# A SwiGLU encoder layer on one core: gate and up as seven block products, gated rows through DRAM, and the way down chunk by chunk

## The chip, the cores and the metric

The kernel runs on one core of a Trainium2 chip. It is one launch that reads its inputs from DRAM and writes eight outputs to DRAM. The metric is the device time of that launch in microseconds. The engines have these names in the profile: PE is TensorE's matmul part and PEld its weight loads, DVE is VectorE, ACT is ScalarE, POOL is GpSimd, and SP is SyncE, which here only issues DMA transfers. Each engine works through its own queue in order; semaphores make one engine wait for another.

## The reference

One layer of an encoder for 1,152 tokens (1,024 of a new stream, 128 of running streams) of width 1,024. Two SwiGLU half steps of hidden width 2,816 stand around a mixer of gated DeltaNet heads and trailing means. Cut to what matters here:

```
def swiglu(x, w_gate, w_up, w_down):
    return (jax.nn.silu(x @ w_gate) * (x @ w_up)) @ w_down

x = x + 0.5 * swiglu(rms_norm(x, norm_ffn1[l]), w_ffn1_gate[l], w_ffn1_up[l], w_ffn1_down[l])
m, s_new, conv_new, pool_new = mixer(rms_norm(x, norm_mix[l]), ...)
x = x + m
x = x + 0.5 * swiglu(rms_norm(x, norm_ffn2[l]), w_ffn2_gate[l], w_ffn2_up[l], w_ffn2_down[l])
...
y_prompt = rms_norm(xp, norm_final)
```

Everything is float32. Both half steps have this same shape, and they take most of the time.

## The kernel before

**Layout.** Channels lie on the 128 partitions and tokens along the free axis. The 1,152 tokens are cut in three chunks: chunk 0 of 512 tokens, chunks 1 and 2 of 320. The residual X of all chunks stays in SBUF in eight blocks of channels (`xk(c, k)`, k from 0 to 7). The hidden width is 22 blocks of 128, numbered f.

**A float32 product from three.** TensorE takes operands of a shorter type here (`fp32r`). Every operand is therefore split exactly into a high and a low part: ACT casts the operand (the high part), and DVE or POOL subtracts the cast from the operand (the low part). `mm3` (L172) then does three matmuls: high by high, high by low, low by high. `load_unit` (L156) does this for weights: it loads a unit of 128 x 1024 values (L160, issued by SP), casts it on ACT (L164), and subtracts on DVE or POOL (L165). The raw units go round a ring of three buffers (`r0` to `r2`), the split ones round four (`s0` to `s3`).

**A SwiGLU half step** is `ffn` (L223). `scale_split` applies the norm's weight to X and splits the result; the factor 1/rms of each token, from `rstd_of` (L178), is applied later. The loop at L294 takes f two at a time. For each f and each chunk, `chunk` (L262) sums 8 k-blocks of three matmuls into one bank of PSUM for gate and as many into another for up, so 48 matmuls of the chunk's width. Then DVE multiplies gate by 1/rms (L275), ACT takes SiLU (L276), DVE multiplies up by 1/rms (L277) and the two together (L278), ACT casts the product (L280) and POOL subtracts (L281). The gated rows of two f stay in SBUF. `down_chunk` (L285) multiplies them by the two units of down weights, for each of the eight output blocks d, and DVE adds half of the sum into X (L292). So X is added to eleven times per chunk and half step, and the down weights are loaded and split once.

**Order.** The program is written in the order in which the engines get their work, and a planner (`Products`, L45) fills the mixer's matmul queue by estimated times. The first half step is called at L337, the mixer follows, and the second half step is called at L1062, with the final norm (`final`, L1051) after each chunk. In the loop the next f's gate and up stand ahead of the previous f's down, so TensorE has work while ACT, DVE and POOL finish a gated row.

Of the kernel before, what the change touches and what calls it, by code (L numbers as in the profile page):

```python
# [28 lines left out]
# columns of the constant matrix  # L29
# [8 lines left out]
def trunk(ctx: ExitStack, tc: tile.TileContext, xin, s0, convst, poolst, cm_in, vec_in, small_in,  # L38
          wg1, wu1, wd1, win, wab_in, wpool_in, wout, wg2, wu2, wd2,
          y_out, pdelta, pconv, ppool, sdelta, sconv, spool, x0_out):  # L40
# [3 lines left out]
    class Products:  # L44
        """the tensor engine, with the time that its queue is filled to"""  # L45
# [32 lines left out]
    X = []  # L78
    for c, (o, n) in enumerate(CHUNKS):
        X.append([xpool.tile([P, KT // 2, n], F32, tag=f"x{c}{i}", name=f"x{c}{i}") for i in range(2)])  # L80

    def x_dma(c, dram, back=False):
        """a chunk of the residual to or from DRAM"""
        n = KT // 2 * CHUNKS[c][1]
        for i in range(2):
            t, d = X[c][i].rearrange("p k n -> p (k n)"), dram[:, i * n:(i + 1) * n]
            SY.dma_start(d if back else t, t if back else d)

    def load_x(c):
        o, n = CHUNKS[c]  # L90
        x_dma(c, xin[:, o * KT:(o + n) * KT])

    def xk(c, k):
        return X[c][k // 4][:, k % 4, :]

    vec = const.tile([P, 32 + 48 + 8 + 1], F32, tag="vec", name="vec")
    SY.dma_start(vec, vec_in)
    cm = const.tile([P, C_END], F32, tag="cm", name="cm")

    def cmat(c):  # L100
        return cm[:, c:c + P]

    ident = cmat(C_ID)
# [8 lines left out]
    main = ctx.enter_context(tc.tile_pool(name="main", bufs=1, side="left"))  # L112
    SIZE = dict(h0h=4096, h0l=4096, h1h=2560, h1l=2560, h2h=2560, h2l=2560, g0=3072, t=2560, rb=1152, g12=3840, spare=1664,
                s0=2048, s1=2048, s2=2048, s3=2048, r0=1024, r1=1024, r2=1024)

    def region(tag, dt=F32):
        """one of the parts in which all phases share what the residual leaves of SBUF"""
        return main.tile([P, SIZE[tag]], dt, tag=tag, name=nm(tag))

    for tag in SIZE:  # L120
        region(tag)

    class Slots:
        """rings of buffers cut from regions"""
# [4 lines left out]
        def place(self, t, *items):  # L129
            o = 0  # L130
            for tag, cols, bufs in items:
                for _ in range(bufs):
                    self.mem.setdefault(tag, []).append(t[:, o:o + cols])
                    o += cols

# [14 lines left out]

    W = {}
# [4 lines left out]
    def load_unit(src, e=None):  # L156
        i = W["i"]
        W["i"] += 1
        raw = region(W["raws"][i % len(W["raws"])])
        SY.dma_start(raw, src)  # L160
        raw = raw.rearrange("p (k c) -> p k c", k=KT)
        w = region(W["splits"][i % len(W["splits"])], F32R).rearrange("p (s k c) -> p s k c", s=2, k=KT)
        hi, lo = w[:, 0], w[:, 1]
        A.copy(hi, raw)  # L164
        (e or V).tensor_sub(lo, raw, hi.bitcast(F32))  # L165
        return hi, lo
# [11 lines left out]
    def rstd_of(c, tmp, r, fast):  # L178
        """1 / rms of each token of a chunk, on all partitions"""
# [9 lines left out]
        if fast:  # L189
            # the tokens on partitions for the root, and back  # L190
# [18 lines left out]
    def scale_split(c, wi, hi, lo):  # L209
        """the norm's weight applied, its 1 / rms left for later"""  # L210
# [5 lines left out]
    def h_rows(t, n, m=KT):  # L216
        return [t[:, k * n:(k + 1) * n] for k in range(m)]

    def h_tiles(c):
        return [h_rows(region(f"h{c}{i}", F32R), CHUNKS[c][1]) for i in "hl"]  # L220

# [1 line left out]
    def ffn(wi, wg, wu, wd, finished):  # L223
        weights(("r1", "r2", "r0"), ("s0", "s1", "s2", "s3"))
        fs = Slots()
        fs.place(region("t"), ("nsq", 512, 3), ("su", 512, 1), ("nacc", 512, 1))
        fs.place(region("rb"), *[(f"rb{c}", CHUNKS[c][1], 1) for c in range(3)])
        for r, cs in (("g0", (0,)), ("g12", (1, 2))):
            fs.place(region(r, F32R), *[(f"{t}{c}", CHUNKS[c][1], 3) for c in cs for t in ("ghi", "glo")])

        def tmp(tag):
            return fs.get(tag, 512)

        first = wi == 0
        order0 = (1, 2, 0) if first else (0, 1, 2)
        H, RB = [None] * 3, [None] * 3
        units0 = None

        for c in order0:
            H[c] = h_tiles(c)  # L240
            RB[c] = fs.get(f"rb{c}", CHUNKS[c][1])
        def norm(c):
            scale_split(c, wi, *H[c])
            rstd_of(c, tmp, RB[c], first)

        if first:
            units0 = [load_unit(wg[0])]
            x_dma(1, xin[:, 512 * KT:832 * KT])
            scale_split(1, wi, *H[1])
            units0.append(load_unit(wu[0]))  # L250
            load_x(2)
            SY.dma_start(cm[:, :P], cm_in[:, :P])
            rstd_of(1, tmp, RB[1], True)
            norm(2)
        else:
            for c in order0:
                scale_split(c, wi, *H[c])
                if units0 is None:
                    units0 = load_unit(wg[0]), load_unit(wu[0])
                rstd_of(c, tmp, RB[c], False)  # L260

        def gate_up(f):  # L262
            g, u = units0 if f == 0 else (load_unit(wg[f]), load_unit(wu[f]))
            out = [None] * 3

            def chunk(c, late=None):
                n = CHUNKS[c][1]
                pg, pu = pt("a")[:, :n], pt("b")[:, :n]
                for ps, (whi, wlo) in ((pg, g), (pu, u)):
                    for k in range(KT):  # L270
                        mm3(ps, whi[:, k, :], wlo[:, k, :], H[c][0][k], H[c][1][k], k == 0, k == KT - 1)
                if late:
                    late()
                sg, su = tmp("nsq")[:, :n], tmp("su")[:, :n]
                V.tensor_mul(sg, pg, RB[c])  # L275
                A.activation(sg, sg, AF.Silu)  # L276
                V.tensor_mul(su, pu, RB[c])  # L277
                V.tensor_mul(sg, sg, su)  # L278
                ghi, glo = fs.get(f"ghi{c}", n), fs.get(f"glo{c}", n)
                A.copy(ghi, sg)  # L280
                G.tensor_sub(glo, sg, ghi.bitcast(F32))  # L281
                out[c] = (ghi, glo)
            return out, chunk

        def down_chunk(c, ws, gs):  # L285
            n = CHUNKS[c][1]
            nf = len(ws)
            for d in range(KT):
                po = pt("cd"[d % 2])[:, :n]
                for i in range(nf):  # L290
                    mm3(po, ws[i][0][:, d, :], ws[i][1][:, d, :], gs[i][c][0], gs[i][c][1], i == 0, i == nf - 1)
                V.scalar_tensor_tensor(xk(c, d), po, 0.5, xk(c, d), ALU.mult, ALU.add)  # L292

        for f in range(0, NF, 2):  # L294
            order = order0 if f == 0 else (0, 1, 2)
            g0, do0 = gate_up(f)
            if f == 0 and not first:
                do0(0)
                g1, do1 = gate_up(f + 1)
                do1(0)  # L300
                for do in (do0, do1):
                    do(1)
                    do(2)
            elif f == 0:
                do0(1)
                do0(2)
                g1, do1 = gate_up(f + 1)
                load_x(0)
                SY.dma_start(cm[:, P:], cm_in[:, P:])
                do1(1)  # L310
                scale_split(0, wi, *H[0])
                do1(2)
                do0(0, lambda: rstd_of(0, tmp, RB[0], True))
                do1(0)
            else:
                for c in order:
                    do0(c)
                g1, do1 = gate_up(f + 1)
            ws = [load_unit(wd[f]), load_unit(wd[f + 1])]
            if f + 2 < NF:  # L320
                if f:
                    for c in order:
                        do1(c)
                for c in order:
                    down_chunk(c, ws, (g0, g1))
            else:
                do1(0)
                down_chunk(0, ws, (g0, g1))
                finished(0, tmp)
                do1(1)  # L330
                do1(2)
                for c in (1, 2):
                    down_chunk(c, ws, (g0, g1))
# [815 lines left out]
```

## Time and profile before

| | |
|---|---|
| Time, median of 3 runs | 2291.96 us (2291.74 to 2292.35) |
| Span of the profiled execution | 2290.1 us |
| Profiled execution's own time | about 1.9 us more than its span, 2292.0 us |
| Instructions | 32,077 |
| DMA | 120.98 MB, mean 53 GB/s |

How to read the rows: a window row gives the stretch in microseconds, then the busy time of each engine with its count of instructions, then the mean granted TensorE clock (1.00 is full speed), the busy share of the DMA engines and the GB/s moved. A timeline row gives start and duration in microseconds, engine, line, operation, output and input by the program's names, the shape, a count, and in brackets the idle time before it with what ended it. A group row gives, behind the shape and the count, total busy time in microseconds with the mean of one in nanoseconds, and then the idle time just ahead with its releasers. Matmuls overlap, so the time that one takes from the engine is the distance between starts.

### The profile page before, as it was taken

Reading aid. Unit: us, or ns where it says so; the run is one execution under the profiler, and the core shown is the slowest. Engines: PE = TensorE matmul, PEld = TensorE weight load, DVE = VectorE, ACT = ScalarE, POOL = GpSimd, SP = SyncE. Lnnn points to the kernel's source line nnn. Section 1 sums busy time; section 2 is a strip of 40 time slices with the busy share of each in tenths; the row PEclk is TensorE's granted clock in tenths of the full one; section 3 lists DMA queues with packets and bytes.
Section 4 is the critical chain, followed back from the end, with each engine's and each line's share of the span. In section 5 each row is a group of like instructions: output and inputs, shape, how many; then the busy total and the mean of one; then the engine's idle time right before and its main releaser. Section 6 shows DMA issues by size and latency. Waiting matters only on the chain. (4 is left out here: it accounts for less than half of the span.)

```text
span 2290.1 us, 32077 instructions
## 1 busy us (share of the span) xinstructions
PE 2233.9 (98%) x13087; PEld 2034.3 (89%) x13087; DVE 1193.8 (52%) x2367; ACT 638.0 (28%) x1246; POOL 346.2 (15%) x384
## 2 busy tenths in 40 slices
PE   8999999999999998999999989999999999999997
PEld 7999999999999987787999978999999999999986
DVE  6443344334443477778687687644433443344345
ACT  6111111111112145544554345411121111111113
POOL 1101000100011002222243332100110011000102
PEclk9999999999999999999999999999999999999998
DMA  4111111111111102111222122111111111111102
GB/s 175 46 44 49 37 45 49 38 37 56 37 37 47 37 30 75 47 57 57 90 71 72 57 82 78 47 56 37 38 48 45 37 37 56 38 37 46 47 10 83
DMA packets 36995, 120.98 MB, mean 53 GB/s; under 512 B 5296, under 2 KB 9264, under 8 KB 36080
## 3 DMA queue, kind: packets, MB, share of 16 engines
q1 hardware_dynamic: 36720, 118.70, 16.1%
q8 instruction: 102, 1.67, 0.3%
q0 software_dynamic: 128, 0.25, 0.1%
q14 instruction: 45, 0.37, 0.1%
HBM read 109.31 MB, written 9.62 MB: 52 GB/s over the span
## 5 line engine op out<-in xcount | busy, mean ns | idle before, releaser
L55 PE MATMUL ps_a<-h0h,s 128*128 128x512 f32 (+1 forms) x1504 | 455.3, 373 | 3.7 <-DVE s L165 2.0
L164 ACT CAST s<-r 128x1024 fp32r<-128x1024 f32 x188 | 195.3, 1050 | 720.7 <-PE ps_d L55 477.8
L281 POOL TENSOR_TENSOR g<-t,g 128x512 fp32r<-128x512 f32 (+1 forms) x132 | 155.8, 1180 | 1460.7 <-ACT g L280 1398.5
L55 PE MATMUL ps_c<-g,s 128*128 128x320 f32 (+1 forms) x1584 | 319.5, 336 | 1.6 <-POOL g L281 1.2
L55 PE MATMUL ps_d<-g,s 128*128 128x320 f32 (+1 forms) x1584 | 318.2, 336 | 0.0
L55 PEld LDWEIGHTS ps_a<-h0h,s 128*128 128x128 f32 x1504 | 276.0, 189 | 43.2 <-issue 2.7
L55 PEld LDWEIGHTS ps_c<-g,s 128*128 128x128 f32 x1584 | 260.9, 188 | 24.4 <-POOL g L281 2.1
L55 PEld LDWEIGHTS ps_d<-g,s 128*128 128x128 f32 x1584 | 261.1, 188 | 20.7
L55 PE MATMUL ps_a<-h0l,s 128*128 128x512 f32 (+1 forms) x752 | 278.5, 370 | 0.0
L277 DVE TENSOR_TENSOR t<-ps_b,rb 128x512 f32<-128x512 f32 (+1 forms) x132 | 73.6, 558 | 363.6 <-PE ps_b L55 363.6
L275 DVE TENSOR_TENSOR t<-ps_a,rb 128x512 f32<-128x512 f32 (+1 forms) x132 | 73.6, 558 | 301.7 <-PE ps_a L55 220.2
L165 DVE TENSOR_TENSOR s<-r,s 128x1024 fp32r<-128x1024 f32 x172 | 209.0, 1225 | 41.4 <-ACT s L164 39.5
L55 PE MATMUL ps_b<-h0h,s 128*128 128x512 f32 x704 | 224.3, 389 | 0.0
L55 PE MATMUL ps_a<-h1h,s 128*128 128x320 f32 x944 | 208.0, 315 | 7.5 <-ACT h1h L213 7.5
L280 ACT CAST g<-t 128x512 fp32r<-128x512 f32 (+1 forms) x132 | 67.8, 513 | 383.9 <-DVE t L278 380.9
L55 PEld LDWEIGHTS ps_a<-h1h,s 128*128 128x128 f32 x944 | 157.9, 191 | 9.6 <-ACT h1h L213 7.5
L55 PE MATMUL ps_b<-h2h,s 128*128 128x320 f32 (+1 forms) x736 | 166.3, 308 | 0.0
L55 PE MATMUL ps_b<-h1h,s 128*128 128x320 f32 x704 | 162.5, 310 | 0.0
L55 PE MATMUL ps_a<-h2h,s 128*128 128x320 f32 x704 | 162.3, 309 | 0.0
L292 DVE SCALAR_TENSOR_TENSOR x<-ps_d,x 128x320 f32<-128x320 f32 (+1 forms) x220 | 116.7, 530 | 85.7 <-PE ps_d L55 85.7
L292 DVE SCALAR_TENSOR_TENSOR x<-ps_c,x 128x320 f32<-128x320 f32 (+1 forms) x220 | 116.7, 531 | 82.6 <-PE ps_c L55 82.6
L55 PEld LDWEIGHTS ps_a<-h0l,s 128*128 128x128 f32 x752 | 142.8, 190 | 18.3 <-issue 0.5
(341 smaller groups left out, 3390.7 us busy)
## 6 DMA issues: line engine op xcount, KB each, us to landing
r<-in_wg SPq DMA_DIRECT2D x44, 512.0 KB, 3.7
r<-in_wu SPq DMA_DIRECT2D x44, 512.0 KB, 3.6
r<-in_wd SPq DMA_DIRECT2D x44, 512.0 KB, 3.6
r<-in_win SPq DMA_DIRECT2D x40, 512.0 KB, 3.6
r<-in_wout SPq DMA_DIRECT2D x16, 512.0 KB, 3.6
x<-in_xin SPq DMA_DIRECT2D x4, 640.0 KB, 7.3
out_y<-x SPq DMA_DIRECT2D x16, 160.0 KB, 1.8
x<-in_xin SPq DMA_DIRECT2D x2, 1024.0 KB, 11.2
```

The lines of the kernel that those rows point to most:

```text
L55: self.put(nc.tensor.matmul(out, lhs, rhs, **k), n / 2400 + .003 if lhs.dtype == F32R else max(n, lhs.shape[-1]) / 600)
L164: A.copy(hi, raw)
L165: (e or V).tensor_sub(lo, raw, hi.bitcast(F32))
L275: V.tensor_mul(sg, pg, RB[c])
L277: V.tensor_mul(su, pu, RB[c])
L280: A.copy(ghi, sg)
L281: G.tensor_sub(glo, sg, ghi.bitcast(F32))
L292: V.scalar_tensor_tensor(xk(c, d), po, 0.5, xk(c, d), ALU.mult, ALU.add)
```

## The change

Gate and up of one f are one product of a 2 x 2 block matrix of weights (rows: gate and up; columns: the two halves of the 1,024 input channels, 4 k-blocks each) and a 2 x 2 block matrix of activations (rows: the halves of the channels; columns: two groups of tokens). Eight block products are replaced by seven products of sums and differences of blocks (Winograd's form). The two groups of tokens are the halves of chunk 0 (pair 0, 256 tokens each) or chunks 1 and 2 (pair 1, 320 each).

- `operands` makes, once per pair and half step, seven activation operands from the normed residual, in place in X, and splits each in high and low part: casts on ACT, subtractions alternately on DVE and POOL. X is overwritten, so it is loaded again later from DRAM.
- `gate_up` runs over f. Per f it loads one gate and one up unit, forms four weight sums of 128 x 512 on POOL, casts and subtracts seven half units (`piece`, ACT and DVE, a ring of seven buffers `O0` to `O6`), and does seven products of 4 x 3 matmuls each, in the order B11, B21, then T4 and B22 of the f before, then T2, T1, T3. ACT copies three sums out of PSUM. The gated rows are cast (ACT), subtracted (POOL) and written to DRAM in both parts (`g_keep`).
- The first f of a half step (3 in the first, 4 in the second, for one pair) still go the old way, `plain`, while operands are made. `beside` makes the operands of the other pair during the first pair's loop.
- `fetch` reads the gated rows of a chunk back into SBUF, and `down` then sums all 22 f of one output block in one bank of PSUM with one add into X. The down weights are loaded and split for each chunk, so three times.
- The constant matrix `cm` is loaded after the first half step, and the four pooling histories are loaded by SP in place of POOL's own queue.

The core of the diff:

```diff
+    def operands(p, wi, RS):
...
+        def split(name, src):
+            t = region(f"{reg}{STEPS.index(name)}", F32R)[:, :8 * n].rearrange("p (s k n) -> p s k n", s=2, k=4)
+            A.copy(t[:, 0], src)
+            turn[0] += 1
+            (V if turn[0] % 2 else G).tensor_sub(t[:, 1], src, t[:, 0].bitcast(F32))
...
+        norm(cs[0])
+        yield op
+        split("B11", l1)
+        split("B21", l2)
+        yield op
+        if p:
+            norm(cs[1])
+            yield op
+        V.tensor_sub(l1, l1, r1)
+        V.tensor_sub(r1, r2, r1)
+        split("B22", r2)
+        yield op
+        V.scalar_tensor_tensor(r2, l1, -1.0, r2, ALU.mult, ALU.subtract)
+        split("T2", r2)
+        split("T1", l1)
+        yield op
+        split("T3", r1)
+        V.scalar_tensor_tensor(l2, r2, -1.0, l2, ALU.mult, ALU.subtract)
+        split("T4", l2)
+        yield op
...
+        def piece(src):
+            t = region(f"O{ring[0] % 7}", F32R)
+            ring[0] += 1
+            hi, lo = t[:, :512], t[:, 512:]
+            A.copy(hi, src)
+            V.tensor_sub(lo, src, hi.bitcast(F32))
...
+        def tail(f, u2, s4, al, be, p1, c2, c3):
+            product(al, piece(u2), "T4", False, True)
+            V.scalar_tensor_tensor(p1, al, -1.0, p1, ALU.mult, ALU.mult)
+            go = gs.get("go", 4, n)
+            A.copy(go[:, 0], p1)
+            G.tensor_sub(go[:, 1], p1, go[:, 0].bitcast(F32))
+            product(be, piece(s4), "B22", False, True)
+            V.tensor_add(c2, c2, be)
+            A.activation(c2, c2, AF.Silu)
+            V.scalar_tensor_tensor(c2, c3, -1.0, c2, ALU.mult, ALU.mult)
+            A.copy(go[:, 2], c2)
+            G.tensor_sub(go[:, 3], c2, go[:, 2].bitcast(F32))
...
+        for i, f in enumerate(fs):
...
+            product(al, piece(g1), "B11", True, True)
+            A.copy(p1, al)
+            product(ga, piece(g2), "B21", True, True)
+            V.tensor_add(p1, p1, ga)
+            A.activation(p1, p1, AF.Silu)
+            G.tensor_add(sA, u1, u2)
+            G.tensor_add(sB, sA, g1)
+            if last:
+                tail(*last)
+            product(al, piece(sB), "T2", False, True)
+            A.copy(c2, al)
+            product(be, piece(sA), "T1", True, True)
+            G.tensor_add(sA, g1, u1)
+            product(al, piece(sA), "T3", False, True)
+            A.copy(c3, al)
+            V.tensor_add(c3, c3, be)
+            G.tensor_add(sB, sB, g2)
+            last = (f, u2, sB, al, be, p1, c2, c3)
+            beside(f)
...
+    def down(c, wd, home):
...
+        for ds in groups:
+            ps = {d: pt("d")[:, :n] for d in ds}
+            for f0, m in cuts:
+                for d in ds:
+                    whi, wlo = load_unit(wd[d][:, f0 * P:(f0 + m) * P])
+                    for i in range(m):
+                        f = f0 + i
+                        mm3(ps[d], whi[:, i, :], wlo[:, i, :], home[f][:, :n], home[f][:, n:], f == 0, f == NF - 1)
+            for d in ds:
+                V.scalar_tensor_tensor(xk(c, d), ps[d], 0.5, xk(c, d), ALU.mult, ALU.add)
...
+    op, homes, fetch = half_step(0, wg1, wu1, wd1, g_keep, 1, 3, None)
+    fetch(1, ["B0", "B1", "B2", "B3", "B4", "B5"])
+    gate_up(0, op, range(NF), wg1, wu1, g_keep)
...
+    x_new(1)
+    x_dma(1, xin)
+    fetch(0, ["B6", "x20", "x21"] + [f"A{i}" for i in range(7)] + ["B0", "B1"])
+    x_new(0)
+    x_dma(0, xin)
+    down(1, wd1, homes[1])
+    fetch(2, ["B2", "B3", "B4", "B5", "B6", "B0"])
+    x_new(2)
+    x_dma(2, xin)
+    down(0, wd1, homes[0])
+    down(2, wd1, homes[2])
...
+    down(0, wd2, homes[0])
+    final(0)
+    fetch(2, ["A2", "A3", "A4", "A5", "A6", "B0", "B1"])
+    down(1, wd2, homes[1])
+    final(1)
...
+    down(2, wd2, homes[2])
+    final(2)
```

In the second half step the pairs go in the order 0, 1.

How the queues stand. ACT before, in the steady loop of the first half step (`s` are split weights, `r` raw ones, `t` the gated product, `g0` and `g12` the gated rows):

```order
L164 CAST s2_145_1544<-r0_144_1542 128x1024
L164 CAST s3_147_1549<-r1_146_1547 128x1024
L276 ACTIVATE t_19_99<-t_19_99 128x512
L280 CAST g0_21_101<-t_19_99 128x512
L276 ACTIVATE t_19_99<-t_19_99 128x320
L280 CAST g12_22_102<-t_19_99 128x320
L164 CAST s0_149_1554<-r2_148_1552 128x1024
L276 ACTIVATE t_19_99<-t_19_99 128x320
L164 CAST s1_151_1559<-r0_150_1557 128x1024
```

ACT now, one f of the half chunks' loop (`O` are half units, `Q` the weight sums, `R` raw weights, `x00` the intermediates and `x01` the gated rows). The line before the copy L345 is the cast of T3's half unit, and the lines after it are those of the next f and of the tail:

```order
L308 CAST O4_462_4501<-Q_344_3238 128x512
L345 COPY x00_342_3236<-ps_a_453_4391 128x256
L308 CAST O5_468_4526<-R0_463_4519 128x512
L308 CAST O6_469_4542<-R0_463_4519 128x512
L348 ACTIVATE x00_342_3236<-x00_342_3236 128x256
L308 CAST O0_470_4561<-R3_452_4388 128x512
L323 CAST x01_343_3237<-x00_342_3236 128x256
L308 CAST O1_471_4579<-Q_344_3238 128x512
L327 ACTIVATE x00_342_3236<-x00_342_3236 128x256
L354 COPY x00_342_3236<-ps_a_453_4391 128x256
L329 CAST x01_343_3237<-x00_342_3236 128x256
```

In place of four casts of whole units there are seven of half units per f, each with the name of a sum or of a raw unit, and they stand among copies and SiLUs that wait for products.

POOL had one line in the loop before, the subtraction L281. Now one f of the same loop has six, the four sums between the subtractions of the gated rows:

```order
L360 TENSOR_TENSOR Q_344_3238<-Q_344_3238,R2_523_5179 128x512
L349 TENSOR_TENSOR Q_344_3238<-R1_536_5312 128x512
L356 TENSOR_TENSOR Q_344_3238<-R2_523_5179,R3_524_5180 128x512
L350 TENSOR_TENSOR Q_344_3238<-Q_344_3238,R0_535_5311 128x512
L324 TENSOR_TENSOR x01_343_3237<-x00_342_3236,x01_343_3237 128x256
L330 TENSOR_TENSOR x01_343_3237<-x00_342_3236,x01_343_3237 128x256
```

So a sum stands behind the gated row's subtraction of an earlier f, and the casts of sums on ACT stand behind POOL's sums.

SP before issued nothing but weights in the loop. Now, where the first half step goes from the half chunks' loop to the way down of chunk 1, it has the last gated rows' stores (L333), the fetches of chunk 0's gated rows (L463, `A3` to `A6`), chunk 0's residual (L109) and the down weights (L154):

```order
L333 DMA g_keep0<-x01_343_3237 256x1x256
L463 DMA A4_618_6154<-g_keep0 128x1024 x2
L463 DMA A5_619_6155<-g_keep0 128x1024 x2
L463 DMA A6_620_6156<-g_keep0 128x1024 x2
L109 DMA x00_623_6181<-in_xin 128x2048
L109 DMA x01_624_6182<-in_xin 128x2048
L154 DMA O6_633_6247<-in_wd1 128x1024
```

The first two units of down weights are issued earlier; the third, `O6_633`, stands behind the fetches and the residual.

More of the change, by code (lines that the diff above doesn't have):

```diff
@@ L214, in scale_split @@
             V.scalar_tensor_tensor(lo[k], xk(c, k), w, hi[k].bitcast(F32), ALU.mult, ALU.subtract)
-    def h_rows(t, n, m=KT):
-        return [t[:, k * n:(k + 1) * n] for k in range(m)]
     def h_tiles(c):
[L220 to L232, printed above, removed]
-        first = wi == 0
[L235 to L241, printed above, removed]
+        n = CHUNKS[c][1]
@@ L262, in gate_up @@
[L262 to L333, printed above, removed]
-                    finished(c, tmp)
@@ L337, in trunk @@
-    ffn(0, wg1, wu1, wd1, lambda c, tmp: None)
-    weights(("r0", "r1"), ("s0", "s1", "s2"))
+            x_new(0)
+            x_dma(0, x_keep)
+            for c in (1, 2):
+                x_dma(c, x_keep, True)
+            scale_split(0, wi, *H[0])
+            units = [load_unit(wg[0]), load_unit(wu[0])]
+            norm(0)
+        for f in range(early):
+            plain(f, units if f == 0 else (load_unit(wg[f]), load_unit(wu[f])), cs, H, RS, fs, gk)
+        op = None
+        for op in operands(lead, wi, RS):
+            pass
@@ new lines, in half_step, with beside, fetch @@
+        nxt = [None, None]
+        def beside(f):
+            if f == early and first:
+                x_new(0)
+                x_dma(0, xin)
+            if f == early + 1:
+                nxt[0] = operands(1 - lead, wi, {})
+            if f > early and nxt[0]:
+                nxt[1] = next(nxt[0], nxt[1])
+        gate_up(lead, op, range(early, NF), wg, wu, gk, beside)
+        for op in nxt[0]:
+            nxt[1] = op
+        homes = {}
+        def fetch(c, where):
+            homes[c] = slots(c, where)
+            for f in range(NF):
+                SY.dma_start(homes[c][f].bitcast(F32), gk[c][f])
@@ L921, in trunk @@
     scale_split(0, 1, *hb[0])
-    rstd_of(0, pair(mt("raw", 512), mt("k", 512, slot=1), mt("q", 512, slot=1)), R[0], False)
-    ahead = region("h1h")
+    rstd_of(0, pair(mt("raw", 512), mt("raw", 512), mt("Xs", 512)), R[0], False)
+    ahead = region("B4")
     z2 = ahead[:, 1536:]
@@ L1043, in trunk @@
                 cur[1:] = e
-    X[0] = [xpool.tile([P, KT // 2, 512], F32, tag=f"x0{i}", name=f"x0{i}r") for i in range(2)]
-    x_dma(0, x0_out)
     SY.dma_start(pconv, cout.rearrange("p t j -> p (t j)"))
```

251 lines of the change are left out of this document (184 added, 67 removed).

## The prediction

> **What bounds the kernel now.** I read the page's totals first, then the stages by windows, then single rows.
>
> ```profile
> span 2290.1 us, 32077 instructions
> PE 2233.9 (98%) x13087; PEld 2034.3 (89%) x13087; DVE 1193.8 (52%) x2367; ACT 638.0 (28%) x1246; POOL 346.2 (15%) x384
> ```
> ```profile
> core 0: us, PE busy (x) PEld busy (x) DVE busy (x) ACT busy (x) POOL busy (x), PEclk, DMA share, GB/s
> 8.00:60.00 52.00, 50.31 (x297) 46.74 (x297) 36.66 (x69) 36.58 (x68) 6.88 (x7) 1.00 0.44 163
> 60.00:830.00 770.00, 769.36 (x4410) 708.64 (x4409) 321.91 (x508) 133.88 (x198) 73.37 (x61) 1.00 0.13 41
> 830.00:1460.00 630.00, 600.54 (x3685) 527.08 (x3684) 480.98 (x1229) 312.27 (x743) 174.18 (x232) 0.99 0.21 67
> 1460.00:2260.00 800.00, 798.52 (x4614) 738.33 (x4613) 334.61 (x528) 140.76 (x211) 78.61 (x67) 1.00 0.13 42
> ```
> The windows 60 to 830 and 1460 to 2260 us are the two SwiGLU half steps, and TensorE never pauses there at a granted clock of 1.00; ACT works 17% and POOL 10% of them. So those stages cost what their matmuls cost, and one spacing row prices everything:
>
> ```profile
> 200.04 0.62 PE L55 MATMUL ps_b<-h0h,s 128*128 128x512 f32 x2
> 200.50 0.39 PE L55 MATMUL ps_b<-h0l,s 128*128 128x512 f32 x1
> 200.72 0.62 PE L55 MATMUL ps_b<-h0h,s 128*128 128x512 f32 x2
> ...
> 203.28 0.46 PE L55 MATMUL ps_a<-h1h,s 128*128 128x320 f32 x2
> 203.57 0.31 PE L55 MATMUL ps_a<-h1l,s 128*128 128x320 f32 x1
> 203.72 0.46 PE L55 MATMUL ps_a<-h1h,s 128*128 128x320 f32 x2
> ```
> Three products of 512 columns start every 0.68 us (0.2267 each), three of 320 every 0.44 (0.1467). The 192 extra columns cost 0.080, so 256 columns come to about 0.120 on the same line (estimate; no row has 256; the upper bound is the 320 row's 0.147, the lower half the 512 row, 0.113).
>
> **The change: what TensorE saves.** Gate and up of one f need 48 products of 512 columns for chunk 0 (10.88 us) and 96 of 320 for the others (14.08). Seven block products are 84: of 256 columns 10.08 us, of 320 columns 12.32. The loops run 40 such f for the pair of half chunks and 41 for chunks 1 and 2, so TensorE's floor falls by 40 x 0.80 + 41 x 1.76 = 104 us. The way down keeps its product count.
>
> **What the loop gives the others.** Each f now brings seven half units to cast and subtract, four weight sums on POOL, two subtractions on POOL, two gated casts, two SiLUs and three PSUM copies. Their prices:
>
> ```profile
> L165 DVE TENSOR_TENSOR s<-r,s 128x1024 fp32r<-128x1024 f32 x172 | 209.0, 1225 | 41.4 <-ACT s L164 39.5
> L280 ACT CAST g<-t 128x320 fp32r<-128x320 f32 x88 | 40.5, 460 | 158.6 <-DVE t L278 155.6
> L280 ACT CAST g<-t 128x512 fp32r<-128x512 f32 x44 | 27.3, 620 | 225.3 <-DVE t L278 225.3
> L278 DVE TENSOR_TENSOR t<-t 128x320 f32<-128x320 f32 x88 | 43.4, 493 | 9.9 <-ACT t L276 1.0 <-DVE t L277 0.5
> L278 DVE TENSOR_TENSOR t<-t 128x512 f32<-128x512 f32 x44 | 30.5, 693 | 5.6 <-ACT t L276 1.2
> ```
> ```profile
> 205.46 1.30 POOL L281 TENSOR_TENSOR g<-t,g 128x512 fp32r<-128x512 f32 x1 [10.09 <-ACT g L280]
> 211.94 0.88 POOL L281 TENSOR_TENSOR g<-t,g 128x320 fp32r<-128x320 f32 x1 [5.18 <-ACT g L280]
> 218.98 1.37 POOL L281 TENSOR_TENSOR g<-t,g 128x320 fp32r<-128x320 f32 x1 [6.16 <-ACT g L280]
> ```
> ACT pays 0.62 for 512 columns, 0.46 for 320 and so 0.41 for 256; DVE 0.69, 0.49, 0.42; POOL 1.30, 0.88, 0.74. Per f of chunks 1 and 2 ACT has 7 x 0.62 + 7 x 0.46 = 7.6 us, POOL 4 x 1.30 + 2 x 0.88 = 7.0, DVE about 7.3: each alone fits in 12.32. Before, POOL only answered ACT and nobody waited. Now the queues make a **ring** (the rows of order above show both queues): the sums (POOL) go to the cast of T3's half unit (ACT), which stands ahead of the copy L345; behind this come, in ACT's own order, the casts of B11 and B21, the SiLU, T4's cast, the first gated cast, B22's cast and the second SiLU; then DVE multiplies (L328), ACT casts (L329), POOL subtracts (L330), and behind that stand the next sums. For chunks 1 and 2, with all four sums ahead: 4 x 1.30 + 0.62 + (4 x 0.62 + 5 x 0.46 + 0.49) + 0.88 = 11.97 us. For the half chunks three sums stand ahead: 3.90 + 0.62 + (2.48 + 2.05 + 0.42) + 0.74 = 10.21. Four hand-offs from engine to engine, 0.08 each, follow from the next rows: ACT ends at 218.90 and POOL begins at 218.98. The rings are then 12.3 and 10.5 us, TensorE's floors 12.3 and 10.1: no slack at all.
>
> ```profile
> 217.86 0.49 DVE L278 TENSOR_TENSOR t<-t 128x320 f32<-128x320 f32 x1
> 218.39 1.22 DVE L165 TENSOR_TENSOR s<-r,s 128x1024 fp32r<-128x1024 f32 x1
> ...
> 218.44 0.46 ACT L280 CAST g<-t 128x320 fp32r<-128x320 f32 x1
> ```
> ```profile
> L640 DVE TENSOR_TENSOR h2h<-rb,cm 128x128 f32<-128x128 f32 x16 | 10.4, 708 | 0.1
> L640 DVE TENSOR_TENSOR t<-rb,cm 128x128 f32<-128x128 f32 x16 | 3.6, 285 | 0.1
> ```
> And the ring stretches. POOL's 320 columns took 1.37 us instead of 0.88 while DVE ran L165 (218.39 to 219.61): 0.49 of it is waiting. The other way round too: L640, the same operation, means 708 ns in one buffer and 285 in another, in the mixer, where POOL is busy. [...]
>
> Seven subtractions of 0.69 us run per f; how many fall into POOL's part of the ring no row shows. The bounds are none and four (those of the sums and B22, which follow POOL's work directly); I take two, 1.4 us: **11.9 us per f for the half chunks, 13.7 for chunks 1 and 2**. Against before: 40 x (11.9 - 10.88) = +41, 41 x (13.7 - 14.08) = -16, together **+25 us**. The saving of 104 is gone in the ring.
>
> **Operands beside the loops.** While one pair runs, the other pair's operands are made:
>
> ```profile
> L165 POOL TENSOR_TENSOR s<-r,s 128x1024 fp32r<-128x1024 f32 x16 | 38.8, 2427 | 39.9 <-ACT s L164 39.2 <-ACT r L454 0.3
> L164 ACT CAST s<-r 128x1024 fp32r<-128x1024 f32 x188 | 195.3, 1050 | 720.7 <-PE ps_d L55 477.8 <-PE ps_a L55 133.8 <-issue 82.8
> L184 ACT ACTIVATE t<-x 128x320 f32<-128x320 f32 x48 | 21.7, 463 | 12.2 <-DVE t L188 9.1 <-PE ps_d L55 1.9 <-DVE x L292 1.0
> ```
> Three of seven splits go to POOL: 3 x 2.43 (1024 columns) + 3 x 3.0 (1280, in proportion) = 16.4 us, straight in the ring. ACT does 7 x 1.05 + 7 x 1.31 + 8 x 0.62 + 16 x 0.46 = 29 us more, a third of it in the ring: **+26**. At nothing if the ring has slack, 60 if all of it and DVE's share counts. The first loop of the first half starts with its own operands not ready: 16 norms x 0.49, four sums and four splits of 1280 columns (1.53 each) are 20 us of DVE; TensorE's plain f cover part: **+8** (0 to 15).
>
> **Hand-overs between loops.** Weights now queue on SP behind other transfers.
>
> ```profile
> r<-in_wg SPq DMA_DIRECT2D x44, 512.0 KB, 3.7
> ```
> ```profile
> 216.13 0.33 SPq L160 DMA_DIRECT2D r<-in_wu  x1
> ```
> ```profile
> 10.00:15.00 5.00, 5.00 (x27) 5.00 (x26) 4.65 (x10) 5.00 (x12) 0.00 (x0) 1.00 1.05 422
> ```
> A filled DMA moves 0.42 MB a us; a unit of 0.52 MB lands 3.7 us after issue, 1.2 of it transfer. From gate_up(0) to down(1) the last gated row goes out about 3 us after the last product (its cast, subtraction and store); behind it SP holds six fetches of 0.52 MB and 2.1 MB of X, and only then the third unit: 3 + 5.24/0.42 + 1.2 + 2.4 = 19 us, +2.3 to split it, less 7.0 that TensorE has of two units (48 x 0.1467): 14. The same sum gives 13 at the first half's gate_up(1) to gate_up(0) (seven fetches of 0.33 MB ahead of the first up weights), 6.5 and 7 at the second half's two, 14 at down(0) to down(1), where the last norm's sums (8 x 0.46 and their adds) stand on TensorE ahead of the next chunk and its stores ahead of the weights, 4 at the next: **+59** (30 to 80). Before, none of these was there: TensorE never paused. Splitting the down weights three times instead of once has TensorE's 3.5 us per unit as cover against ACT's 1.05 and DVE's 1.22, and costs nothing; without cover it would be 1.2 a unit. Inside a loop SP issues two weights and two gated stores per f, 4 x 0.33 = 1.3 us of 12, with the raw weights of two f in their buffers: 0, and one landing, 3.7 us, for any f whose weights stand behind a late store. The mixer keeps its plan; its four pooling histories move from POOL's queue to SP's, 1.3 us of issues beside TensorE's work (0, up to 10 if SP holds them behind weights).
>
> **Sum.** 25 + 26 + 8 + 59 = 118 us on the profiled execution: span 2290.1 plus 1.9 around it is 2292.0, the median of the runs. Forecast 2410.
>
> **Rivals.**
> - Faster: TensorE stays the bound, since the casts run up to seven half units ahead and the ring closes inside its floor. That decides if POOL's sums are never held by DVE and the ring of 12.3 is as short as counted. Then -104, operands hidden, hand-overs 59 and start 8: 2255. For it, each engine alone is under 62% busy; against it, the 1.37 row, and a ring with no slack. Chance 0.15.
> - [...] Chance 0.15.
> - Four subtractions in the ring: 13.3 and 15.1 us per f, +97 +41 = 138 in place of 25: 2523. For it, sums and subtractions follow each other directly; against it, DVE may finish its subtraction while ACT holds the ring. Chance 0.20.
> - That the block products are not fewer is out: the counts per f are 84 for 96.
>
> **How the numbers follow.** The forecast has 0.50. Its own terms spread it over 2340 to 2480; the range 2270 to 2530 takes in the port's case and nearly all of the four-subtraction case, and leaves out most of the fast one. A measurement tells 0.2% (4.6 us) from no change. Faster 0.14 (nearly all of the first rival), same 0.03 (its upper edge and the port's lower one), slower 0.83.
>
> **What would show it.** Right: in the loops TensorE busy 85 to 90%, its idle time ended by DVE (half units) and ACT, POOL's sums over 1.30 us, period 11.9 and 13.7; pauses of 5 to 20 us at the hand-overs ended by a split of weights. [...] A spacing of 256 columns near 0.147 would make TensorE's floor of the half chunks 84 x 0.147 = 12.3 us, 0.4 over their ring: +16 in 40 f.

## The result, and the profile after

| | before | after |
|---|---|---|
| Time, median | 2291.85 us (2287.96 to 2292.35, 4 runs) | 2480.38 us (2478.73 to 2482.89, 4 runs) |
| Span of the profiled execution | 2290.1 us | 2477.0 us |

The ratio is 1.083, with a 95% interval of 1.081 to 1.084: 8% slower. The forecast was 2410, in a range of 2270 to 2530. The page's totals after:

```profile
span 2477.0 us, 37268 instructions
PE 2203.6 (89%) x14055; PEld 2049.2 (83%) x14055; DVE 1433.6 (58%) x2575; ACT 1066.7 (43%) x2163; POOL 843.2 (34%) x758
```

TensorE fell from 98% to 89% busy, and no other engine is over 58%. So something waits in a circle (a ring), or TensorE waits at the ends of loops. The period of the loops is read from one instruction that each f has once on ACT, the copy L345. The rows give the count, the three durations in nanoseconds (least, median, greatest), and the start of the first and of the last in microseconds. First the steady part of the loop over chunks 1 and 2, then that of the half chunks in the first and in the second half step:

```profile
L345 ACT COPY x<-ps_a x12: 417/420/421, 179.5 to 330.8; 128x320 f32<-128x320 f32 x12
L345 ACT COPY x<-ps_a x17: 363/365/367, 420.1 to 619.0; 128x256 f32<-128x256 f32 x17
L345 ACT COPY x<-ps_a x8: 363/366/369, 1739.2 to 1823.2; 128x256 f32<-128x256 f32 x8
```

The periods are 151.3/11 = 13.75 us, 198.9/16 = 12.43 and 84.0/7 = 12.0 (12.3 over both). TensorE needs 12.32 and 10.08 (84 starts at 0.1467 and 0.120 us; without the sums, below, the loops ran at both). The same rows where the other pair's operands are made beside the loop, in the first and in the second half step:

```profile
L345 ACT COPY x<-ps_a x6: 402/418/426, 68.9 to 165.7; 128x320 f32<-128x320 f32 x6
L345 ACT COPY x<-ps_a x10: 364/372/376, 1599.1 to 1739.2; 128x256 f32<-128x256 f32 x10
```

Five periods take 96.8 us where 68.8 would be steady, and nine take 140.1 in place of 110.7: 57 us more. At a change of loop TensorE's timeline shows the pause in brackets, and the windows beside it show the DMA engines full (share 1.03, 407 GB/s) and the granted clock:

```profile
637.69 1.60 PE L55 MATMUL ps_c<-A,O 128*128 128x256 f32 x12
639.13 6.62 PE L55 MATMUL ps_d<-B,O 128*128 128x320 f32 x44
663.30 0.90 PE L55 MATMUL ps_d<-B,O 128*128 128x320 f32 x2 [17.55 <-ACT O L156]
```
```profile
639.00:657.00 18.00, 6.75 (x47) 6.48 (x45) 0.84 (x2) 0.82 (x2) 1.37 (x2) 0.80 1.03 407
662.00:667.00 5.00, 3.34 (x11) 2.94 (x12) 3.36 (x4) 2.82 (x3) 0.00 (x0) 0.50 0.78 283
667.00:672.00 5.00, 5.00 (x36) 5.00 (x35) 1.00 (x2) 0.83 (x1) 0.00 (x0) 1.00 0.68 226
```

The seven pauses of over 2.4 us at such changes are 11.5, 17.6, 10.9, 8.9, 2.8, 8.9 and 2.7 us in order of time, together 63. So the 186.9 us of longer span are: gate and up 40 x (12.3 - 10.88) + 41 x (13.75 - 14.08) = 43; the slow first turns of the two loops 57; pauses at the changes 63; and some 24 for the rest, a mixer that is about 5 us longer and work at a granted clock of 0.50 after pauses among it.

**One turn of the ring.** One period of chunks 1 and 2 on SP, POOL, ACT and DVE (cut to the links):

```profile
252.09 0.33 SPq L339 DMA_DIRECT2D R<-in_wu  x1
```
```profile
254.32 0.87 POOL L330 TENSOR_TENSOR x<-x,x 128x320 fp32r<-128x320 f32 x1 [1.52 <-ACT x L329]
256.10 1.47 POOL L349 TENSOR_TENSOR Q<-R 128x512 f32<-128x512 f32 x1 [0.91 <-DMA R<-in_wu]
257.65 1.30 POOL L350 TENSOR_TENSOR Q<-Q,R 128x512 f32<-128x512 f32 x1
258.91 1.29 POOL L360 TENSOR_TENSOR Q<-Q,R 128x512 f32<-128x512 f32 x1
260.16 1.29 POOL L356 TENSOR_TENSOR Q<-R,R 128x512 f32<-128x512 f32 x1
```
```profile
261.49 0.62 ACT L308 CAST O<-Q 128x512 fp32r<-128x512 f32 x1 [4.38 <-POOL Q L356]
262.01 0.42 ACT L345 COPY x<-ps_a 128x320 f32<-128x320 f32 x1
262.33 1.14 ACT L308 CAST O<-R 128x512 fp32r<-128x512 f32 x2
264.11 0.47 ACT L348 ACTIVATE x<-x 128x320 f32<-128x320 f32 x1 [0.64 <-DVE x L347]
264.49 0.60 ACT L308 CAST O<-R 128x512 fp32r<-128x512 f32 x1
```
```profile
251.37 0.69 DVE L309 TENSOR_TENSOR O<-R,O 128x512 fp32r<-128x512 f32 x1
...
265.12 0.69 DVE L309 TENSOR_TENSOR O<-R,O 128x512 fp32r<-128x512 f32 x1
```

Read it round: DVE's subtraction of T4's half unit (251.37 to 252.06) is the last reader of a raw up unit. SP issues the next load into that buffer at 252.09, and POOL's first sum starts at 256.10, ended by that load. Four sums follow, then ACT's cast of T3's half unit (ACT idled 4.38 us for it), the copy, two casts, a SiLU, T4's cast, and at 265.12 the same subtraction again, 13.75 us after the first. The gated rows' subtraction on POOL, L330, ended at 255.19, 0.91 us before it mattered.

The half chunks close elsewhere:

```profile
487.79 0.74 POOL L330 TENSOR_TENSOR x<-x,x 128x256 fp32r<-128x256 f32 x1 [1.40 <-ACT x L329]
489.15 1.68 POOL L360 TENSOR_TENSOR Q<-Q,R 128x512 f32<-128x512 f32 x1 [0.63 <-DVE O L309]
```
```profile
494.23 1.11 DVE L309 TENSOR_TENSOR O<-Q,O 128x512 fp32r<-128x512 f32 x1 [4.22 <-ACT O L308]
```

The sum L360 is written over the sum that T2's half unit is made from, so it waits for DVE's subtraction of that half unit, 0.63 us after L330 has ended, and is then itself, at 1.68 us, 0.39 longer than the 1.29 of its neighbours. Later in the same turn DVE's subtraction of T3's half unit takes 1.11 us in place of 0.69, while POOL runs the sum L350 (493.50 to 494.79). The load closes this loop too in some turns: in the four of 13.1 to 13.3 us that stand among those of 11.9 to 12.6, POOL's first sum L349 waits 1.1 to 1.3 us for the up weights.

### The profile page after: what moved, and what is told of

The parts are those of the page before. It is cut to its first block, busy times and chain, and to the rows that moved or that the text cites. A ratio compares the mean times of both kernels' runs of the same rounds, so it can differ in the third digit from the quotient of the medians.

```text
span 2477.0 us, 37268 instructions
## 1 busy us (share of the span) xinstructions
PE 2203.6 (89%) x14055; PEld 2049.2 (83%) x14055; DVE 1433.6 (58%) x2575; ACT 1066.7 (43%) x2163; POOL 843.2 (34%) x758
## 5 line engine op out<-in xcount | busy, mean ns | idle before, releaser
L55 PE MATMUL ps_a<-A,O 128*128 128x256 f32 (+2 forms) x3344 | 585.8, 319 | 82.5 <-ACT x L354 53.9
L55 PEld LDWEIGHTS ps_a<-A,O 128*128 128x128 f32 x3344 | 490.1, 197 | 115.9 <-ACT x L354 60.9
L309 DVE TENSOR_TENSOR O<-Q,O 128x512 fp32r<-128x512 f32 x324 | 268.7, 848 | 383.5 <-ACT O L308 381.9
L55 PE MATMUL ps_a<-B,O 128*128 128x320 f32 (+1 forms) x2224 | 396.6, 320 | 62.6 <-ACT x L354 50.0
L55 PE MATMUL ps_d<-B,O 128*128 128x320 f32 (+1 forms) x2328 | 408.6, 331 | 33.3 <-ACT O L156 26.4
L55 PEld LDWEIGHTS ps_a<-B,O 128*128 128x128 f32 x2224 | 347.9, 192 | 78.6 <-ACT x L354 59.5
L55 PEld LDWEIGHTS ps_d<-B,O 128*128 128x128 f32 x2328 | 364.9, 191 | 53.7 <-ACT O L156 26.9
L308 ACT CAST O<-Q 128x512 fp32r<-128x512 f32 x324 | 193.4, 618 | 345.9 <-POOL Q L356 329.2
L55 PE MATMUL ps_d<-A,O 128*128 128x512 f32 (+1 forms) x1176 | 239.1, 362 | 11.0 <-ACT O L156 10.4
L55 PEld LDWEIGHTS ps_d<-A,O 128*128 128x128 f32 x1176 | 205.1, 192 | 40.0 <-ACT O L156 11.5
L324 POOL TENSOR_TENSOR x<-x,x 128x320 fp32r<-128x320 f32 (+1 forms) x81 | 75.8, 936 | 271.6 <-ACT x L323 269.4
L55 PEld LDWEIGHTS ps_c<-B,O 128*128 128x128 f32 x984 | 148.7, 189 | 11.7 <-ACT O L308 11.7
L55 PE MATMUL ps_c<-A,O 128*128 128x256 f32 x960 | 131.4, 286 | 12.1 <-ACT O L308 11.5
L349 POOL TENSOR_TENSOR Q<-R 128x512 f32<-128x512 f32 x81 | 114.4, 1413 | 71.4 <-DMA R<-in_wu 57.6
L360 POOL TENSOR_TENSOR Q<-Q,R 128x512 f32<-128x512 f32 x81 | 121.4, 1499 | 37.4 <-DVE O L309 37.4
L55 PEld LDWEIGHTS ps_c<-A,O 128*128 128x128 f32 x960 | 123.2, 194 | 12.9 <-ACT O L308 11.7
```

The lines of the kernel that those rows point to most:

```text
L55: self.put(nc.tensor.matmul(out, lhs, rhs, **k), n / 2400 + .003 if lhs.dtype == F32R else max(n, lhs.shape[-1]) / 600)
L308: A.copy(hi, src)
L309: V.tensor_sub(lo, src, hi.bitcast(F32))
L324: G.tensor_sub(go[:, 1], p1, go[:, 0].bitcast(F32))
L349: G.tensor_add(sA, u1, u2)
L360: G.tensor_add(sB, sB, g2)
```

## The experiments

Each was timed beside the kernel before, which took 2288 to 2290 us there; where no number of runs is given, the time is one execution's.

### One more raw buffer

```diff
-            rg, ru = region(f"R{2 * i % 4}"), region(f"R{2 * i % 4 + 1}")
+            rg, ru = region(f"R{2 * i % 4}"), region(f"R{(1, 3, 4)[i % 3]}")
```

To make room for the buffer, the kernel's `dynamic_dma_scratch_size` is halved; the two later runs with a fifth buffer do the same.

> One more raw buffer, so that the up weights go round three buffers and gate's round two. Theory (load ring): in the loop of chunks 1 and 2 the up weights' buffer comes free only with T4's subtraction (252.06 us in the profile of after), they land at 256.1, and the four sums, T3's cast and T4's next cast follow: 13.75 us round. With a third buffer the load is ahead, and POOL's own order closes the ring; its gated subtraction ended at 255.19, so 0.9 us less: 12.8 us per f of chunks 1 and 2, 12.1 as before for the half chunks, about 30 us off the total (2450). Rival (the ring of the prediction, over the gated rows' subtraction on POOL): the load is only the last of two that end together; period 13.7, total within 5 us of 2480.

It took 2440.8 us. The two loops' steady rows:

```profile
L345 ACT COPY x<-ps_a x9: 418/420/423, 204.4 to 305.8; 128x320 f32<-128x320 f32 x9
L345 ACT COPY x<-ps_a x16: 367/367/368, 409.3 to 589.8; 128x256 f32<-128x256 f32 x16
```

The periods are 101.4/8 = 12.68 us and 180.5/15 = 12.03. Chunks 1 and 2 lost 1.07 us per f, a little more than the 0.9 expected, and the half chunks lost the occasional 13 us that a late load had given them. POOL's first sum no longer waits for the load there, so the load ring is shown for chunks 1 and 2. POOL's order changed with the buffer too (the first sum now stands ahead of both gated rows' subtractions, the second between them), so the 1.07 us is the load and the new order together.

### No weight sums

```diff
-            G.tensor_add(sA, u1, u2)
-            G.tensor_add(sB, sA, g1)
...
-            product(al, piece(sB), "T2", False, True)
+            product(al, piece(g1), "T2", False, True)
```

> Leaves out the four weight sums on POOL; the products T2, T1, T3 and B22 take raw halves of the weights in their place, so the outputs are other numbers. Theory (the sums stand in the ring that paces the loop): periods fall to TensorE's floors, 10.1 to 10.5 us per f of the half chunks and 12.3 to 12.6 of chunks 1 and 2, and the total to 2300 to 2350. Rival (casts, subtractions and copies on ACT and DVE pace the loop by themselves): periods fall by less than 0.5 us, total above 2440.

It took 2300.8 us. TensorE's floors are reached to the hundredth, 135.5/11 = 12.32 us and 171.4/17 = 10.08:

```profile
L345 ACT COPY x<-ps_a x12: 427/427/427, 154.5 to 290.0; 128x320 f32<-128x320 f32 x12
L345 ACT COPY x<-ps_a x18: 372/372/373, 356.2 to 527.6; 128x256 f32<-128x256 f32 x18
```

ACT, DVE and their 7 casts and subtractions per f fit. So every ring that paces the loops goes through the sums on POOL or through what they hold up, and they cost 180 us in all, the slow iterations beside the operands included.

### The weight sums on DVE

```diff
-            G.tensor_add(sA, u1, u2)
-            G.tensor_add(sB, sA, g1)
+            V.tensor_add(sA, u1, u2)
+            V.tensor_add(sB, sA, g1)
```

and the same for the two others.

> The four weight sums move from POOL (1.29 us each) to DVE (0.69 each). Theory (the sums' length and their holding each other up with DVE's subtractions make the ring): the ring shortens by 2.4 us and more, so chunks 1 and 2 come to TensorE's floor, 12.3 to 12.6, the half chunks to 10.1 to 10.8; total about 2350. Rival (DVE becomes the bound of the half chunks: 7 x 0.69 + 5 x 0.41 + 4 x 0.69 = 9.6 us of work behind waits, of a floor of 10.1): half chunks stay at 11 to 12, chunks 1 and 2 at 12.3; total about 2400.

It took 2329.2 us, 151 less than the changed kernel. The rows give 73.7/6 = 12.28 us and 173.1/17 = 10.18:

```profile
L345 ACT COPY x<-ps_a x7: 425/426/428, 217.4 to 291.1; 128x320 f32<-128x320 f32 x7
L345 ACT COPY x<-ps_a x18: 372/373/377, 351.5 to 524.6; 128x256 f32<-128x256 f32 x18
```

The theory held and the rival fell: the loop's arithmetic fits if the sums are 0.69 us long and not 1.29; on DVE the four lines of sums took 0.69 to 0.77 us in the mean. How much of this is the sums' own length and how much that they no longer stand beside DVE's subtractions (L360 at 1.68 us) is not separated by this run.

### Fetches after the first group of the way down

```diff
+        for j, ds in enumerate(groups):
+            if late and j == 1:
+                late()
...
+    def late():
+        fetch(0, ["B6", "x20", "x21"] + [f"A{i}" for i in range(7)] + ["B0", "B1"])
+        x_new(0)
+        x_dma(0, xin)
+    down(1, wd1, homes[1], late)
```

> In the first half step the fetches of chunk 0's gated rows and its residual are issued after the first group of chunk 1's way down in place of before it. Theory (the third unit of down weights waits on SP behind 5.2 MB): the pause of TensorE between the half chunks' loop and the way down falls from 17.5 us to under 5, and about 12 us go from the total, unless the way down of chunk 0 then waits for its rows. Rival (the unit waits for its buffer, which the loop's last half unit holds): the pause stays above 12 us.

It took 2471.1 us, 9.3 less. The pause after the half chunks' loop:

```profile
647.88 0.72 PE L55 MATMUL ps_d<-B,O 128*128 128x320 f32 x3 [2.72 <-ACT O L156]
...
667.37 0.56 PE L55 MATMUL ps_d<-B,O 128*128 128x320 f32 x2 [3.33 <-ACT O L156]
```

It fell from 17.55 us to 2.72, and 3.33 came back one group later, where the 22 fetches now stand in one block. So at this change the weights' place on SP makes the pause.

### The other pair's operands after the loop

```diff
-        gate_up(lead, op, range(early, NF), wg, wu, gk, beside)
-        for op in nxt[0]:
+        gate_up(lead, op, range(early, NF), wg, wu, gk)
...
+        for op in operands(1 - lead, wi, {}):
```

> The changed kernel with the other pair's operands made after the loop in place of beside it. Theory (the slow first iterations, 82.8 us for four in the first half step and 128.7 for eight in the second, come from the operands): all iterations but the first come to 13.75 and 12.2, which takes 25 to 30 us from each loop, and TensorE pauses 30 to 40 us at each change of pair, so the total is 2470 to 2500. Rival (they come from the loop's start itself, its own late operands and loads): the first iterations stay at 17 to 23 us, and the total rises to 2530 and more.

It took 2461.9 us, 18.5 less than with the operands beside the loop, and less than either theory said. The loops' first iterations:

```profile
L345 ACT COPY x<-ps_a x7: 404/420/426, 70.1 to 159.7; 128x320 f32<-128x320 f32 x7
L345 ACT COPY x<-ps_a x11: 364/366/367, 1576.5 to 1702.7; 128x256 f32<-128x256 f32 x11
```

Six periods take 89.6 us (7 over steady, in the first two) and ten take 126.2 (3 over ten of 12.3). So 10 of the 57 us belong to the loops' starts, and 47 to the operands. Done between the loops they cost some 29 us (47 less 18.5), less than when they are mixed into a loop that has no slack.

### The operands' subtractions all on DVE

```diff
-            (V if turn[0] % 2 else G).tensor_sub(t[:, 1], src, t[:, 0].bitcast(F32))
+            V.tensor_sub(t[:, 1], src, t[:, 0].bitcast(F32))
```

> The changed kernel with all subtractions of the operands' splits on DVE. Theory of the prediction (POOL's three splits of 2.43 or 3.0 us stand straight in the ring): the slow iterations of both loops lose 10 to 16 us together, total 2465. Rival (the norm's and splits' work on ACT and DVE makes them slow): less than 5 us, or a loss, since DVE gets 8 us more.

It took 2464.6 us, 15.8 less. The slow iterations, to be read beside those of the changed kernel:

```profile
L345 ACT COPY x<-ps_a x6: 404/420/428, 69.5 to 155.0; 128x320 f32<-128x320 f32 x6
L345 ACT COPY x<-ps_a x10: 362/372/379, 1579.8 to 1712.7; 128x256 f32<-128x256 f32 x10
```

They take 85.5 and 132.9 us in place of 96.8 and 140.1, 18.5 less together. So moving POOL's six splits is worth 16 us by the total and 18.5 by the rows, with the 8 us that DVE takes on already paid, and of the 47 us some 29 are left for what ACT and DVE do for the operands. In the changed kernel POOL's splits were longer than the 2.43 and 3.0 us reckoned, 21 us for the six:

```profile
L236 POOL TENSOR_TENSOR B<-x,B 128x1280 fp32r<-128x1280 f32 x6 | 22.6, 3764 | 17.5 <-ACT B L234 17.5
L236 POOL TENSOR_TENSOR A<-x,A 128x1024 fp32r<-128x1024 f32 x6 | 19.6, 3268 | 18.4 <-ACT A L234 18.3
```

### A buffer of its own for the fourth sum

```diff
-            G.tensor_add(sB, sB, g2)
+            s4 = s4s[:, i % 2 * 512:(i % 2 + 1) * 512]
+            G.tensor_add(s4, sB, g2)
```

> The fourth weight sum (for B22) gets a buffer of its own in place of being written over the sum that T2's half unit is made from. Theory (in the half chunks' loop POOL waits for DVE's subtraction of T2's half unit before it may write the sum L360, 0.63 us, and is held 0.39 us by the next one): that link opens and the half chunks' period falls from 12.0 to 12.4 to about 11.4; chunks 1 and 2, which wait for the load of the up weights, stay at 13.7; total about 2450. Rival (the ring of the prediction, closed by the gated rows' subtraction on POOL, L330): the sum stands behind that subtraction anyway, periods within 0.2 us of before, total within 8 us of 2480.

It took 2518.2 us, a miss for both: the half chunks' period rose to 202.3/15 = 13.49 us.

```profile
L345 ACT COPY x<-ps_a x16: 362/365/368, 426.6 to 628.9; 128x256 f32<-128x256 f32 x16
```
```profile
498.58 0.52 SPq L333 DMA_DIRECT2D g_keep<-x  x1
499.19 0.56 SPq L339 DMA_DIRECT2D R<-in_wu  x1
```
```profile
497.73 0.82 POOL L324 TENSOR_TENSOR x<-x,x 128x256 fp32r<-128x256 f32 x1 [2.33 <-ACT x L323]
...
503.15 1.28 POOL L349 TENSOR_TENSOR Q<-R 128x512 f32<-128x512 f32 x1 [2.46 <-DMA R<-in_wu]
```

With the wait gone the sum moved from the first to the last of the four in POOL's order, and, as the rows read, a longer ring took over: the up load (499.19) stands on SP right behind the store of the first gated row, which starts when POOL's subtraction L324 ends (498.55), and POOL's first sum waits 2.46 us for that load. The run doesn't tell the two theories apart. It shows that the loop has several rings of nearly one length, and that opening one can lengthen another.

### Gated subtractions on DVE, with the fifth raw buffer

```diff
-            G.tensor_sub(go[:, 1], p1, go[:, 0].bitcast(F32))
+            V.tensor_sub(go[:, 1], p1, go[:, 0].bitcast(F32))
```

and the same for the second gated row.

> The kernel with one more raw buffer (2440.8 us, 12.68 and 12.03 us per f), and the gated rows' subtractions moved from POOL to DVE. Theory (T2's half unit closes the ring, not the gated rows): periods within 0.3 us of 12.68 and 12.03, since DVE gets 0.8 to 1.0 us more per f; total 2430 to 2450. Rival (the ring of the prediction, closed by the gated rows' subtraction L330): the ring opens, chunks 1 and 2 come to 12.32 and the half chunks to 11.2 or less; total about 2390.

It took 2426.5 us. The rows give 123.9/10 = 12.39 us and 179.6/15 = 11.97:

```profile
L345 ACT COPY x<-ps_a x11: 418/419/421, 173.5 to 297.4; 128x320 f32<-128x320 f32 x11
L345 ACT COPY x<-ps_a x16: 366/367/367, 400.8 to 580.4; 128x256 f32<-128x256 f32 x16
```

The total is 14 us below the 2440.8 and 3.5 below the theory's range. The half chunks stay where they were, as the theory had it, but the traces show that this doesn't decide between the two. First the half chunks with the fifth buffer alone, then with the subtractions moved:

```profile
500.86 1.18 POOL L330 TENSOR_TENSOR x<-x,x 128x256 fp32r<-128x256 f32 x1
502.00 1.74 POOL L360 TENSOR_TENSOR Q<-Q,R 128x512 f32<-128x512 f32 x1
```
```profile
503.42 0.97 DVE L330 TENSOR_TENSOR x<-x,x 128x256 fp32r<-128x256 f32 x1 [0.47 <-ACT x L329]
504.31 1.28 DVE L309 TENSOR_TENSOR O<-Q,O 128x512 fp32r<-128x512 f32 x2
505.06 1.68 POOL L360 TENSOR_TENSOR Q<-Q,R 128x512 f32<-128x512 f32 x1 [0.96 <-DVE O L309]
```

With the fifth buffer the sum L360 follows the gated row's subtraction on POOL without a gap, where in the changed kernel it waited 0.63 us for DVE. After the move the same subtraction stands without a gap ahead of T2's half unit on DVE, for which L360 waits. So it is part of the turn in both kernels, at 1.18 and at 0.97 us, and which link closes the half chunks' ring stays open. Chunks 1 and 2 come near TensorE's 12.32, which is 0.07 from where the rival put them and 0.29 from where they had been, so for them the run decides less.

### All transfers spread out, with the sums on DVE

```diff
+    bring = fetch(1, ["B0", "B1", "B2", "B3", "B4", "B5"])
+    gate_up(0, op, range(NF), wg1, wu1, g_keep, lambda f: next(bring, None))
...
+                    whi, wlo = load_unit(wd[d][:, f0 * P:(f0 + m) * P])
+                    next(late, None)
...
+    def late3():
+        yield from pairs(fetch(1, ["A0", "A1"]))
+        final(0)
+        yield
+        yield from fetch(2, ["A2", "A3", "A4", "A5", "A6"])
```

`fetch` is a generator here that issues one row at a time, and `down` advances `late` once per unit of weights.

> The weight sums on DVE, and every transfer that is not weights spread out: a row of the gated rows per f inside the following loop, or per unit of down weights inside the way down, the residual and the final norm of a chunk likewise after the first units. Theory (fetches and residual ahead of the weights on SP make the pauses at the hand-overs): the five pauses of 8 to 17 us fall to under 5 each, about 40 us from the 2329 of the kernel with only the sums on DVE: 2290, a tie with the kernel before. Rival (the pauses come from the last tail of a loop and from the buffers that it holds): pauses stay, total above 2320. Second rival (the spread transfers slow the loops' own weights): pauses fall but the loops' periods rise above 10.3 and 12.5.

It took 2253.96 us (2251.95 to 2260.0, 4 runs), 75 less than with the sums on DVE alone, twice what was expected. The ratio to the kernel before is 0.984 (0.983 to 0.986). None of the seven changes of loop has a pause of over 2.4 us any more.

### The same with the operands' subtractions on DVE

> As the one with all transfers spread, and the splits of the other pair's operands subtracted by DVE alone (1.22 and 1.53 us each) where POOL had three of seven (2.43 and 3.0). Theory (POOL's long subtractions hold DVE and the gated rows up while operands are made): 5 to 15 us less than the other. Rival (DVE, which has the sums now, is the one that is short while operands are made): equal or up to 10 us more.

It took 2242.25 us (2239.36 to 2244.81, 4 runs), 11.7 less than the one above: 0.979 of the kernel before (0.978 to 0.981), so about 2% less. Its steady loops and its change from the half chunks to the way down:

```profile
L345 ACT COPY x<-ps_a x9: 427/428/429, 186.5 to 285.3; 128x320 f32<-128x320 f32 x9
L345 ACT COPY x<-ps_a x15: 372/376/377, 372.7 to 516.3; 128x256 f32<-128x256 f32 x15
```
```profile
547.15 0.71 PE L55 MATMUL ps_d<-B,O 128*128 128x320 f32 x3 [2.05 <-ACT O L156]
```

The periods are 12.35 and 10.26 us, and the pause that was 17.55 is 2.05. When the loops run near TensorE's floor and nothing that they hang on is late, the seven products bring 47 of their 104 us.

## Why the prediction came out as it did, step by step

- **What bounds, and TensorE's saving of 104 us: right.** The spacing of 256 columns, estimated at 0.120 us, is 1.44/12 = 0.120 at the end of the loop (the twelve products from 637.69 to 639.13), and without the sums both loops ran at the floors that the prediction gave, 12.32 and 10.08.
- **A ring of ACT and POOL eats the saving: right; its size nearly, its closing link wrong.** Forecast were 11.9 and 13.7 us per f, measured 12.3 and 13.75, which makes gate and up 43 us longer and not 25. The step "behind that stand the next sums", over the gated rows' subtraction L330, is the one that failed: in the changed kernel L330 had ended before POOL's next sum could start, by 0.91 us in chunks 1 and 2 and by 0.63 in the half chunks. In chunks 1 and 2 POOL waits for the load of the up weights, which waits for T4's subtraction: the third buffer took 1.07 us out of 13.75. In the half chunks it waits for DVE's subtraction of T2's half unit, in some turns for the load as well. That is read from the rows; no run shows it by itself, since opening that link made the turn longer, and L330 moved to DVE stayed in the turn. That 13.7 came so near to 13.75 is luck: the load latency (4.01 us from the issue at 252.09 to POOL's first sum at 256.10), which the prediction put at nothing inside a loop ("one landing" at most, for a late store), filled the place of the two held subtractions.
- **Two subtractions held, 1.4 us per f: too much.** That two of DVE's subtractions hold POOL for their whole length was the author's estimate, and no run shows it. The half chunks' turn shows 0.39 us on POOL's L360 and 0.42 on DVE's subtraction of T3's half unit, that of chunks 1 and 2 0.18 on L349. The rows show more such pairs, each longer beside the other engine's work: L360 took 1.68 us at 489.15 beside DVE's subtractions (488.26 to 489.68) and 1.29 at 258.91, where DVE ran nothing; and of the sixteen L640 before, four took 1.4 to 2.4 us while POOL ran L165, L525 or L784 (the longest, 2.42 us, from 1371.45, beside an L165 of 2.39 from 1371.34), and made the mean of 708 ns, the others about 0.28. What makes them longer no run shows. Nor does one show the port's case, to which the prediction's range and chances refer; the periods were 12.3 and 13.75 us.
- **Operands beside the loop, 26 us: the term that was mis-sized most, 47 measured.** Of POOL's splits, put at 16.4, 16 to 18.5 came back when they moved; that is near in part by chance, since they took 21 us on POOL, and DVE took on 8. Of the rest a third of ACT's 29 us was taken as falling into the ring; 29 us did, as much as all of ACT's, DVE's share included. The late start of the first loop was sized right, 8 us against 7; the second loop's 3 were not in the sum.
- **Hand-overs, 59 us: right, 63 in pauses.** The 14 of the first half step's way down, whose sum is written out, measured 17.55; the 13 at its change of pair 11.48; the second half step's 6.5, 7, 14 and 4 measured 10.94, 8.87, 11.62 (in two pauses) and 2.65. The total is nearer than its parts. The cause (fetches and residual ahead of weights on SP) is shown by the moved fetch for the first of these, and for the others only by the run that spread all transfers at once. What the prediction didn't have is the granted clock after such pauses: 0.50 from 373.14 to 380.10 us, 0.51 from 663.30 to 667.00, and 0.50 from 1862.03 to 1868.30, 2173.87 to 2179.00 and 2307.27 to 2312.10, behind the five longest.
- **The three loads of the down weights: hidden, as said.** The first half step's ways down took 298 us from 639.1 to 937.2, for 275 of matmuls by their spacings, and the 17.55 us of the pause are most of the rest.
- **The forecast of 2410 was 70 us short; the span's increase of 186.9 is 69 over the 118 of the sum:** 18 in the loops' period, 21 in the operands beside them, 2 in the starts, 4 in the pauses, and the 24 of the rest, for which the sum has no term. The likeliest case was the right one; of the rivals, the four held subtractions came nearest to the total (2523), with periods that the profile doesn't show.

## What to carry to other kernels

Before TensorE is given less to do, list what each in-order queue does per turn and follow the rings, loads into reused buffers among them: three engines that were each 50 to 56% busy in the half chunks' loop (400 to 625 us) made a ring longer than TensorE's turn. Work that only one slow engine does inside such a ring is worth moving to a faster one that is busier (the sums took 1.29 us on POOL and 0.69 to 0.77 on DVE, and the move took off 151 us), and what was put beside a loop without slack cost more than between the loops (47 us against some 29). A block of transfers issued ahead of the next loop's weights stopped TensorE for up to 17.55 us; issued one row per turn, it left the turns within 0.2 us of TensorE's floors (12.35 and 10.26 against 12.32 and 10.08).

## What the hardware showed beyond that

After a pause of 17.55 us TensorE's granted clock was 0.50 from 662 to 667 us, with the next matmul at 663.30, and then 1.00 again (the windows above); the first products after another pause of 8.87 us took 6.85 us for 18 of 512 columns (2173.87 to 2180.72), 0.38 each at a mean granted clock of 0.62, where the twelve behind them (2180.72 to 2183.44) take 0.227 at 1.00. Those 18 so took 2.8 us more, and the 3.7 us at 0.51 after the longer pause cost about 1.8 (estimate, 0.49 of 3.7): these two pauses cost 2 to 3 us more than their length. When the transfers were spread out the total fell by 75 us although the pauses that went added to about 60; how much of the difference the clock makes up, no run shows.

```profile
2173.87 7.01 PE L55 MATMUL ps_d<-A,O 128*128 128x512 f32 x18 [8.87 <-ACT O L156]
2180.72 2.88 PE L55 MATMUL ps_d<-x,O 128*128 128x512 f32 x12
```
